# Small transfers of the attention stage issued by GpSimd in place of SyncE, in a trunk step of three-pass float32 products

## The chip, the cores and the metric

The kernel runs on one core of a Trainium2 chip. The metric is the device time of one launch in microseconds (us). PE is TensorE, PEld its weight loads, DVE is VectorE, ACT is ScalarE, POOL is GpSimd and SP is SyncE, which does nothing but issue transfers (DMAs) and wait. Each engine works through its own instructions in the order in which they stand; an instruction that waits holds up all that stand behind it on that engine.

## The reference

One inference step of two layers for 256 prompt tokens and 8 sample tokens that share the weights: attention and a gated MLP with a short convolution, then a state-space layer (S5) and such an MLP again. The change lies in the attention, which is cut down here to what matters:

```python
q, k, v = qkv_project(h, w_qkv, pos)          # partial rotary on q and k
for g, (win, dil) in enumerate(((128, 1), (512, 4), (2048, 16))):
    k_all = concat([cache_k[g], k[:, :, g]])  # prompt rows: no cache
    v_all = concat([cache_v[g], v[:, :, g]])
    o, lse = dilated_attend(q[:, :, g], k_all, v_all, idx, dil, win // dil)
o = merge_by_denominator(outs, lses)          # over the three groups
return o @ w_o, new_rows                      # the new k and v are outputs too
```

There are 8 heads in each of 3 groups, of 128 channels. The rotated keys and the values of all tokens are outputs.

## The kernel before

All activations lie transposed: channels on the 128 partitions, the 264 tokens along the free dimension. The weights stream through in chunks of eight 128x128 blocks (512 KB). SP loads a chunk (`wraw`, line 175), ACT rounds it to its high part (`whi`, line 162), DVE subtracts to get the rest (`wlo`, line 163), and PE makes three products of each block (lines 202 to 204), 24 to a chunk. There are four buffers for `wraw` and three each for `whi` and `wlo`.

The QKV product runs over the heads: first the keys of a head (three tiles, one for each group g), then the next head's queries, then the head's values. Work on a finished tile is put off by some chunks of weights (`later`), so that it comes between the big products; a scheduler then sets the final order on each engine.

- A finished key or query tile: DVE scales it out of PSUM (`qkv`, line 437) and shuffles 32 rows of it (`sw`, line 443). POOL makes the rotary from that in three operations (lines 449 to 451), which I call the rope. A query's rope ends with a copy `qe` (line 454) that PE reads (line 481); a key's with a small product `qk` (line 522). PE multiplies prompt queries and keys at lines 639 and 640, and its order there is fixed.
- Line 457 stores the rotated key tile to `out_kv` (132 KB), 24 times.
- The sample rows of a head: 24 dot products on DVE give `sc` (line 497). They are laid out anew through DRAM: `sc` is written to `sd` (line 505) and read back as `ss` on 8 partitions (line 510). DVE takes their maximum (`mgs`, line 536), the softmax follows, and the weights `ss` go back the same way: written to `pd` (line 554), read as `pk` on 128 partitions (line 597) for the sums over the cached values (lines 619 and 621). Each of the four is 12 KB, and each read waits for its write to land. There are 8 of each.
- In the background, a few small operations to each chunk, DVE and POOL make tables for the state-space layer (`z_room`, line 912).

Of the kernel before, what the change touches and what calls it, by code (L numbers as in the profile page):

```python
"""One inference step of the dilated-attention / S5 / ConvFFN trunk on one core.

All activations are held transposed: channels on the partitions, the 264 tokens (256 prompt, 8 sample) on
the free dimension.  Weights stream through in blocks of [128 x 128] and are the stationary operand.  A
float32 product is carried by three float32r passes: each operand is split exactly into a high part H
(float32r) and the rest L, and H*H + H*L + L*H is accumulated in PSUM.
"""
# [59 lines left out]
def order_grouped(mts, nk, first):  # L67
    """(k, m) blocks: the first `first` M-tiles k-outer, the others one after the other."""
    out = [(k, m) for k in range(nk) for m in mts[:first]]
    out += [(k, m) for m in mts[first:] for k in range(nk)]  # L70
    return out


def qkv_mtiles():
    """Keys of a head, the next head's queries, then the head's values."""
    seq = [(0, 0)]
    for h in range(H):
        seq += [(1, h)] + ([(0, h + 1)] if h + 1 < H else []) + [(2, h)]
    return [(which * G + g) * H + h for which, h in seq for g in range(G)]
# [24 lines left out]
class Put:  # L104
    """Notes calls to an engine for later."""
# [8 lines left out]
class Pin:  # L114
    """Calls to an engine that keep their place in its queue."""
# [8 lines left out]
class Kern:  # L124
# [12 lines left out]
    # ---------------------------------------------------------------- work put off by some chunks of weights  # L137
# [10 lines left out]
    # ---------------------------------------------------------------- helpers  # L148
# [16 lines left out]
    def ensure(self, i):  # L165
        """Load and split the weight chunks up to number i of the whole stream."""
# [13 lines left out]
    def gemm(self, name, order, nk, rhs, evac, lag=0):  # L180
        """Accumulate all blocks of `order`; rhs(k) -> (H, L) moving operands; evac(m, psum).
        The first output is taken out of PSUM `lag` chunks late, and at most two per chunk while catching up."""
# [31 lines left out]
    def ready(self, lst, k):  # L214
        """lst[k], running the put-off work until it is there."""
        while k >= len(lst) or lst[k] is None:
            self.pump()
        return lst[k]

    # ---------------------------------------------------------------- norms  # L220
    def rstd_mean(self, parts, warm=0):
        """-1/2 (mean of squares + eps) of every token, tokens on the partitions: [88, 3] in PSUM."""
# [11 lines left out]
    def rstd_root(self, mh):  # L234
        """2/3 of 1/sqrt(-2 mh): the bit-shift estimate, a step of third and a step of second order."""
# [18 lines left out]
    def rstd_spread(self, w):  # L254
        """[88, 3] -> a PSUM tile with 3/2 of every token's value on all partitions."""
        nc = self.nc
        ps = self.ps()
        for b in range(3):
            nc.tensor.matmul(
                ps[:, b * TB : (b + 1) * TB], w[:, b : b + 1].to_broadcast([TB, P]), self.ident15,  # L260
                start=True, stop=True,
            )
        return ps[:, 0:NT]

    def warm(self, n):
        """Keeps the tensor engine's clock up over a wait: n products that nothing reads."""
# [8 lines left out]
    def rstd_soon(self, acc):  # L275
        """Puts 1/rms of the squares in acc off into the coming chunks; returns the tile that will hold it."""
# [13 lines left out]
    def squares(self, st, x):  # L290
        """st: list with the running sum of squares (made here) and the tile still to be added."""
# [10 lines left out]
    def yevac(self, ys, gi):  # L302
        """Takes a sub-layer's output out of PSUM, times the post-norm's gain; sums its squares."""
# [10 lines left out]
    def reload(self, src, wait):  # L314
        """The residual, loaded tile by tile in the coming chunks."""
# [11 lines left out]
    def operand(self, x, gi, k):  # L327
        """H/L parts of x*g (not yet scaled by 1/rms); the L part is returned as a function."""
# [10 lines left out]
    def residual(self, ys, xs, sq, keep, gi):  # L339
        """x += rms_norm(y)*g tile by tile; then the next sub-layer's operand (gain gi), its squares, the store.  # L340
        Returns rhs(k) and the tile for 1/rms."""
# [45 lines left out]
    # ---------------------------------------------------------------- constants  # L387
# [18 lines left out]
    # ---------------------------------------------------------------- attention  # L406
    def attention(self, ap, rhs, rget):
        """Returns the list that will hold the split o^T tiles, one per head."""
# [16 lines left out]
        def both(what, h, fn):  # L425
            """Runs fn when the second of its two conditions is met."""
# [21 lines left out]
        def rope(which, g, h, t, sw):  # L448
# [7 lines left out]
            else:  # L456
                self.later(2, lambda: nc.sync.dma_start(O["kv"][0, g, h], t))
# [17 lines left out]
    def sample_q(self, ap, st, h, g):  # L475
        """The 8 sample queries, each on 16 partitions; scores of the cached keys, 8 to a partition."""
# [27 lines left out]
        def write():  # L504
            nc.sync.dma_start(self.sd[h].rearrange("b k g e -> (b k) (g e)"), sc.rearrange("p g e -> p (g e)"))
            self.later(2, read)

        def read():
            ss = ap.tile([NS, 16, G, 8], F32, tag="ss", name=self.nm("ss"), bufs=2)
            nc.sync.dma_start(ss, self.sd[h])  # L510
# [7 lines left out]
    def sample_new(self, ap, st, h, g):  # L518
        """Products of the sample queries with their own new keys."""
# [6 lines left out]
    def sample_softmax(self, ap, st, h):  # L526
        """Softmax weights of the sample queries over the three groups' cached and new keys."""
# [19 lines left out]
        def fin():  # L547
# [6 lines left out]
            nc.sync.dma_start(self.pd[h], ss)  # L554
# [7 lines left out]
    def merge_exp(self, ap, n, tag, mg):  # L562
        """exp(SCALE*(group max - joint max)); mg is [n, groups] or [n, blocks, groups]"""
# [14 lines left out]
    def merge(self, ap, n, tag, e, l, h):  # L578
        """Merge weight of each group over head 0's sum of that group (as the reference divides)."""
# [13 lines left out]
    def sample_out(self, ap, st, h):  # L593
        """Sum of the cached and new values with the softmax weights."""
        nc, I = self.nc, self.I
        pk = ap.tile([P, G, 8], F32, tag="pk", name=self.nm("pk"), bufs=2)
        nc.sync.dma_start(pk.rearrange("p g e -> p (g e)"), self.pd[h].rearrange("b k g e -> (b k) (g e)"))
# [36 lines left out]
    def prompt_scores(self, ap, st, h, g):  # L634
        """Masked scores of one group and their exponentials (against the group's maximum)."""
# [40 lines left out]
    def prompt_out(self, ap, st, h, os_):  # L676
        """P transposed group by group, and o^T accumulated over the groups."""
# [6 lines left out]
        def tr(g):  # L684
            # column blocks: (keys 0, queries 0), (keys 0, queries 1), (keys 1, queries 1)
# [23 lines left out]
    # ---------------------------------------------------------------- ConvFFN  # L709
    def ffn_prep(self, fp, l):  # L710
        """Convolution weights, and the part of the sample rows' convolution that the stored rows give."""
# [67 lines left out]
    # ---------------------------------------------------------------- S5  # L779
    def s5_setup(self, p):  # L780
        """What the state-space layer needs of every state: decay, phase, powers of a.  SN small steps at a time."""
# [20 lines left out]
        def exp(out, x):  # L802
            """e**x for x clamped to [-87, 88], to float32's accuracy."""
# [19 lines left out]
        # sin and cos: reduce to [-pi, pi], take a quarter of the angle, double twice  # L823
# [30 lines left out]
        # powers a**1..a**4: pw[:, 0] real, pw[:, 1] imaginary, pw[:, 2] minus imaginary  # L854
# [7 lines left out]
        # (a - 1) / lambda  # L862
# [17 lines left out]
        # unit phase w of a**4, its powers w**0..w**7 and w**0, w**8, .., w**56  # L880
# [37 lines left out]
    def s5_prep(self, p):  # L918
        """Chunk operators of the state-space layer (4 steps at once), kept in DRAM until they are used."""
# [14 lines left out]
        def finish(j):  # L934
            """Input operators with (channel, step) rows; Re(c a**k bbar) with k = 3 - step."""
# [20 lines left out]
        def finish2(j):  # L956
            """Operators from step s to step t of a chunk: Re(c a**(t - s) bbar) for s <= t."""
# [11 lines left out]
        def load_bc(j):  # L969
            """b and c of four pairs of groups: [p, (b_re b_im c_re c_im), t, 16]"""  # L970
# [14 lines left out]
        for j in range(KD):  # L985
# [6 lines left out]
            # phase tables w**i, i = 0..63  # L992
# [23 lines left out]
            for ri in range(2):  # L1016
                # re: c_re a_re - c_im a_im;  minus im: c_re (-a_im) - c_im a_re
# [15 lines left out]
    def s5(self, p, rhs, rget):  # L1033
# [9 lines left out]
        for ri in range(2):  # L1043
            # a * (initial sample state)
# [9 lines left out]
        def front(j, ps):  # L1054
            """u tile in (step, chunk) order, and through DRAM to (channel, step) rows."""
# [31 lines left out]
        def inject(j, up, u4, op, e, d0):  # L1087
            """What each chunk adds to the state."""
# [12 lines left out]
        def scan(j, up, u4, e, d0, pj):  # L1101
            """Rotate each chunk's share back by the phase, scan with the real decay, rotate again."""
# [88 lines left out]
    # ---------------------------------------------------------------- the step  # L1191
    def run(self):
# [18 lines left out]
        def ffn_layer(l, rhs, rget, keep, nxt):  # L1211
            with ExitStack() as s:
# [8 lines left out]
                def gpool(m):  # L1221
                    """Space for the last gated tiles is that of the state-space layer's preparation."""
# [39 lines left out]
    def first(self, ap, src):  # L1262
        """The first sub-layer's operand, straight from the input."""
# [32 lines left out]
# -------------------------------------------------------------------- host: layouts only  # L1296
# [11 lines left out]
def chan(a):  # L1308
    """[..., channels] -> [channel % 128, ..., channel // 128]"""
# [3 lines left out]
def constants():  # L1313
# [15 lines left out]
    # shift[(i c s'), t, (c s)]: 1 where s' = 3 - t + s  # L1329
# [6 lines left out]
def host_in(a):  # L1336
# [25 lines left out]
    def pl(v):  # L1362
        """[128 groups, 64, ...] -> [128 = (group % 2, state), 64 = group // 2, ...]"""
# [10 lines left out]
    # c of two groups side by side, each on its own group's rows: [j, p, t, (re im), (group, 16)]  # L1374
# [19 lines left out]
def host_out(o):  # L1394
# [8 lines left out]
    def unpl(v):  # L1403
        """[128, 64, ...] -> [128 groups, 64, ...]"""
# [28 lines left out]
```

## Time and profile before

| | |
|---|---|
| median of three runs | 2557.86 us |
| the three runs | 2555.21, 2557.86, 2563.43 us |
| span of the profiled execution | 2555.1 us |
| PE busy | 2469.9 us (97%) |
| DVE, ACT, POOL busy | 1817.1, 1159.4, 830.0 us |

The page gives the profiled execution by its span from the first to the last instruction, 2555.1 us; the shortest of the three runs is 2555.21 us, so next to nothing lies around it. A wait is read as "engine line waited for: us in total, times, longest us". In a row of instructions the bracket at the end is the idle time of the engine just before, and what ended it. The attention stage is roughly the first 530 us.

### The profile page before, as it was taken

The page shows a single profiled execution, that of the slowest core. Times are in us where ns is not written, and L with a number is a line of the kernel's source. Part 1 is how long each engine was busy: PE and PEld are TensorE (multiplying, and loading weights), DVE is VectorE, ACT ScalarE, POOL GpSimd, SP SyncE. Part 2 cuts the span into 40 slices and gives each one's busy share as a digit, 9 for nine tenths or more (in the row PEclk, how much of TensorE's full clock was granted, in tenths as well). Part 3 has the DMA queues.
Part 4 walks back from the last instruction along what each step waited for, and adds up shares of the span by engine and source line. Part 5 has one row for each costly group of instructions (what it writes and reads, how often), then busy time and mean ns, then how long its engine had stood idle before and what let it go on. Part 6 is the DMA issues. An engine that isn't in the chain of part 4 may idle for free.

```text
span 2555.1 us, 52974 instructions
## 1 busy us (share of the span) xinstructions
PE 2469.9 (97%) x20998; PEld 2440.6 (96%) x20998; DVE 1817.1 (71%) x3490; ACT 1159.4 (45%) x1754; POOL 830.0 (32%) x1153
## 2 busy tenths in 40 slices
PE   8999999999999999999999988999999999999997
PEld 8999998999999999999999988999999999999997
DVE  6787998778988887764445878445977777764444
ACT  5344433445555555443334333444655545543332
POOL 6333347344899990011003465102100000011001
PEclk9999999999999999999999999999999999999999
DMA  7666666666666665566556677555655555566553
GB/s 274 218 234 220 210 216 203 202 213 218 202 217 217 207 217 189 182 205 199 182 181 213 212 248 240 184 181 168 198 180 179 181 181 182 182 205 200 181 182 117
DMA packets 186874, 512.14 MB, mean 200 GB/s; under 512 B 39281, under 2 KB 68993, under 8 KB 186369
## 3 DMA queue, kind: packets, MB, share of 16 engines
q1 hardware_dynamic: 141808, 457.89, 54.2%
q0 software_dynamic: 7968, 26.71, 3.3%
q10 hardware_dynamic: 36848, 24.16, 3.2%
q8 instruction: 164, 2.69, 0.4%
q14 instruction: 86, 0.70, 0.1%
HBM read 469.80 MB, written 38.88 MB: 199 GB/s over the span
## 4 chain that ended last, share of the span: by engine, by line
PE 77%; DVE 11%; issue 4%; DMA 3%; ACT 2%; POOL 1%; ACTq 1%; SPq 0%; DVEq 0%; POOLq 0%
PE ps L202 25%; PE ps L204 25%; PE ps L203 24%; DVE wlo L163 4%; DMA yb<-y 1%; DVE C L744 1%; ACT whi L162 1%; DVE ac L621 1%; DVE act L367 1%; DMA ident<-in_ident 1%; ACTq L945 0%; POOL qkv L449 0%; DMA y<-yb 0%; DVE z_room L912 0%; DVE act L335 0%
## 5 line engine op out<-in xcount | busy, mean ns | idle before, releaser
L204 PE MATMUL ps<-act,wlo 128*128 128x264 f32 x6176 | 1763.6, 286 | 30.2 <-DVE wlo L163 30.0
L202 PE MATMUL ps<-act,whi 128*128 128x264 f32 x6176 | 1771.1, 288 | 10.6 <-ACT whi L162 8.3
L203 PE MATMUL ps<-act,whi 128*128 128x264 f32 x6176 | 1760.3, 285 | 10.0 <-DVE act L335 9.8
L163 DVE TENSOR_TENSOR wlo<-wraw,whi 128x1024 fp32r<-128x1024 f32 (+1 forms) x775 | 994.2, 1283 | 555.7 <-ACT whi L162 554.6
L162 ACT ACTIVATE whi<-wraw 128x1024 fp32r<-128x1024 f32 (+1 forms) x775 | 815.9, 1055 | 1024.7 <-PE ps L203 800.5
L204 PEld LDWEIGHTS ps<-act,wlo 128*128 128x128 f32 x6176 | 1168.7, 189 | 36.9 <-DVE wlo L163 36.8
L202 PEld LDWEIGHTS ps<-act,whi 128*128 128x128 f32 x6176 | 1166.1, 189 | 16.3 <-ACT whi L162 9.1
L203 PEld LDWEIGHTS ps<-act,whi 128*128 128x128 f32 x6176 | 1169.2, 189 | 13.0 <-DVE act L335 12.2
L294 POOL TENSOR_TENSOR acc<-acc,sq 128x264 f32<-128x264 f32 x112 | 111.3, 993 | 672.8 <-ACT sq L300 670.3
L736 POOL COPY ckeep<-U 128x10 f32<-128x10 f32 x172 | 64.4, 375 | 652.5 <-DVE U L735 651.4
L744 DVE SCALAR_TENSOR_TENSOR C<-U,cw,C 128x255 f32<-128x255 f32 (+1 forms) x344 | 187.7, 547 | 0.7 <-ACT C L738 0.7
L735 DVE TENSOR_TENSOR U<-ps,rstd 128x264 f32<-128x264 f32 x172 | 73.2, 430 | 72.2 <-PE ps L204 71.8
L738 ACT ACTIVATE C<-U,cw 128x264 f32<-128x264 f32 x172 | 102.1, 596 | 17.6 <-DVE U L735 13.1
L449 POOL TENSOR_TENSOR qkv<-qkv,cs 32x264 f32<-32x264 f32 x48 | 57.3, 1194 | 148.7 <-DVE sw L443 47.4
L121 POOL TENSOR_TENSOR z_e<-z_pa,z_pb 128x256 f32<-128x256 f32 x64 | 73.1, 1142 | 5.0
L621 DVE SCALAR_TENSOR_TENSOR ac<-vc,pk,ac 128x128 f32<-128x128 f32 x184 | 69.0, 375 | 2.2
L497 DVE CUSTOM_DVE_ANT_0 junk<-kc,qx 128x128 f32<-128x128 f32 x192 | 58.4, 304 | 1.4
L660 ACT ACTIVATE S<-S,nmg 128x128 f32<-128x128 f32 (+1 forms) x48 | 21.5, 447 | 82.0 <-DVE nmg L655 82.0
L451 POOL TENSOR_TENSOR qkv<-qkv,sw 32x264 f32<-32x264 f32 x48 | 56.4, 1176 | 3.4
L121 POOL TENSOR_TENSOR z_pa<-z_bc,z_tab 128x256 f32<-128x256 f32 x64 | 55.9, 874 | 2.4
L121 POOL TENSOR_TENSOR z_pb<-z_bc,z_tab 128x256 f32<-128x256 f32 x64 | 53.6, 838 | 0.0
L749 ACT ACTIVATE C<-C 128x264 f32<-128x264 f32 x86 | 35.7, 415 | 34.1 <-DVE C L744 30.4
(213 smaller groups left out, 1698.5 us busy)
## 6 DMA issues: line engine op xcount, KB each, us to landing
wraw<-in_w_up SPq DMA_DIRECT2D x344, 512.0 KB
wraw<-in_w_down SPq DMA_DIRECT2D x172, 512.0 KB
wraw<-in_w_qkv SPq DMA_DIRECT2D x143, 512.0 KB
wraw<-in_w_glu SPq DMA_DIRECT2D x64, 512.0 KB
wraw<-in_w_in SPq DMA_DIRECT2D x32, 512.0 KB
kc<-in_kc SPq DMA_DIRECT2D x24, 512.0 KB
vc<-in_vc SPq DMA_DIRECT2D x24, 512.0 KB
wraw<-in_w_o SPq DMA_DIRECT2D x16, 512.0 KB
```

The costliest lines, as they stand in the source:

```text
L121: return lambda *a, **k: self.tc.keep_in_program_order(getattr(self.eng, name)(*a, **k))
L162: self.nc.scalar.activation(hi, src, AF.Copy)
L163: self.nc.vector.tensor_tensor(lo, src, hi.bitcast(F32), op=ALU.subtract)
L202: nc.tensor.matmul(o, hi[:, c], xh, start=first, stop=False)
L203: nc.tensor.matmul(o, hi[:, c], xl, start=False, stop=False)
L204: nc.tensor.matmul(o, lo[:, c], xh, start=False, stop=last)
L294: nc.gpsimd.tensor_tensor(st[0], st[0], st[1], op=ALU.add)
L621: nc.vector.scalar_tensor_tensor(ac, vcs[g][:, e], w, ac, op0=ALU.mult, op1=ALU.add)
L735: nc.vector.tensor_tensor(u, ps[:, 0:NT], rget(), op=ALU.mult)
L736: nc.gpsimd.tensor_copy(keep[:, m, :], u[:, NP - 2 : NT])
L738: nc.scalar.activation(c, u, AF.Identity, bias=cw[:, 3, m : m + 1], scale=cw[:, 2, m : m + 1])
L744: nc.vector.scalar_tensor_tensor(c[:, s:NP], u[:, 0 : NP - s], cw[:, j, m : m + 1], c[:, s:NP], op0=ALU.mult, op1=ALU.add)
```

## The change

Five lines go from SP to POOL. The store of a new key (line 457) is also no longer put off by two chunks, but stands right behind the rope. Comments and docstrings are gone as well. Stores of values (line 462) and all big loads stay on SP.

```diff
             else:
-                self.later(2, lambda: nc.sync.dma_start(O["kv"][0, g, h], t))
+                nc.gpsimd.dma_start(O["kv"][0, g, h], t)
                 self.later(3, lambda: self.prompt_scores(ap, st, h, g))
                 self.sample_new(ap, st, h, g)
...
         def write():
-            nc.sync.dma_start(self.sd[h].rearrange("b k g e -> (b k) (g e)"), sc.rearrange("p g e -> p (g e)"))
+            nc.gpsimd.dma_start(self.sd[h].rearrange("b k g e -> (b k) (g e)"), sc.rearrange("p g e -> p (g e)"))
             self.later(2, read)
...
-            nc.sync.dma_start(ss, self.sd[h])
+            nc.gpsimd.dma_start(ss, self.sd[h])
...
-            nc.sync.dma_start(self.pd[h], ss)
+            nc.gpsimd.dma_start(self.pd[h], ss)
...
-        nc.sync.dma_start(pk.rearrange("p g e -> p (g e)"), self.pd[h].rearrange("b k g e -> (b k) (g e)"))
+        nc.gpsimd.dma_start(pk.rearrange("p g e -> p (g e)"), self.pd[h].rearrange("b k g e -> (b k) (g e)"))
```

SP has 998 rows before and 942 after, POOL 1140 and 1196. PE's order is the same, tile names aside. The numbers behind names count buffers and differ between the two kernels.

On SP, the first place where a stored key stands among the weight loads, the keys of head 0 (`qkv_694`, `qkv_738`, `qkv_742` are its groups 0, 1, 2). Before:

```order
L175 DMA wraw_799<-in_w_qkv 128x1024
L457 DMA out_kv<-qkv_694 128x264
L457 DMA out_kv<-qkv_738 128x264
L175 DMA wraw_852<-in_w_qkv 128x1024
L457 DMA out_kv<-qkv_742 128x264
L175 DMA wraw_897<-in_w_qkv 128x1024
```

And of the change:

```order
L175 DMA wraw_757<-in_w_qkv 128x1024
L797 DMA z_room<-in_lre 128x64
L797 DMA z_room<-in_lim 128x64
L797 DMA z_room<-in_ldt 128x64
L175 DMA wraw_802<-in_w_qkv 128x1024
L175 DMA wraw_854<-in_w_qkv 128x1024
L175 DMA wraw_897<-in_w_qkv 128x1024
```

The weight loads follow one another with no store between them.

On POOL, the keys of head 6: the rope of group 0, the tables of the state-space layer, the rope of group 1. Before:

```order
L451 TENSOR_TENSOR qkv_5824<-qkv_5824,sw_5826 32x264
L522 TENSOR_TENSOR qk_5856<-qkv_5236,qkv_5824 128x8
L912 TENSOR_TENSOR z_room<-z_room 128x64x2
L912 TENSOR_TENSOR z_room<-z_room 128x128 x2
L912 TENSOR_TENSOR z_room<-z_room 128x64x2
L912 TENSOR_TENSOR z_room<-z_room 128x256 x2
L912 TENSOR_TENSOR z_room<-z_room 128x64x4
L912 TENSOR_TENSOR z_room<-z_room 128x256
L449 TENSOR_TENSOR qkv_5957<-qkv_5957,cs 32x264
```

And of the change:

```order
L451 TENSOR_TENSOR qkv_5824<-qkv_5824,sw_5826 32x264
L457 DMA out_kv<-qkv_5824 128x264
L522 TENSOR_TENSOR qk_5857<-qkv_5237,qkv_5824 128x8
L912 TENSOR_TENSOR z_room<-z_room 128x64x2
L912 TENSOR_TENSOR z_room<-z_room 128x128 x2
L505 DMA sd_111<-sc_5406 128x24
L912 TENSOR_TENSOR z_room<-z_room 128x64x2
L912 TENSOR_TENSOR z_room<-z_room 128x256 x2
L912 TENSOR_TENSOR z_room<-z_room 128x64x4
L912 TENSOR_TENSOR z_room<-z_room 128x256
L510 DMA ss_6065<-sd_111 8x384
L449 TENSOR_TENSOR qkv_5958<-qkv_5958,cs 32x264
```

The store, the write of `sd` and the read of `ss` now stand on POOL ahead of the rope of group 1, and five table operations stand between the write and the read.

On DVE, the same place: the maximum `mgs` of head 6 among the work on its group 1 key (`qkv_5957` before, `qkv_5958` after). Before:

```order
L163 TENSOR_TENSOR wlo_5929<-wraw_5927,whi_5928 128x1024
L437 TENSOR_TENSOR qkv_5957<-ps_5874,rstd_528 128x264
L443 STREAM_SHUFFLE sw_5959<-qkv_5957 32x264
L163 TENSOR_TENSOR wlo_5987<-wraw_5985,whi_5986 128x1024
L536 TENSOR_REDUCE mgs_6198<-ss_6064 8x3
L163 TENSOR_TENSOR wlo_6032<-wraw_6030,whi_6031 128x1024
```

And of the change:

```order
L163 TENSOR_TENSOR wlo_5930<-wraw_5928,whi_5929 128x1024
L437 TENSOR_TENSOR qkv_5958<-ps_5875,rstd_528 128x264
L536 TENSOR_REDUCE mgs_6198<-ss_6065 8x3
L443 STREAM_SHUFFLE sw_5960<-qkv_5958 32x264
L163 TENSOR_TENSOR wlo_5988<-wraw_5986,whi_5987 128x1024
L163 TENSOR_TENSOR wlo_6033<-wraw_6031,whi_6032 128x1024
```

The maximum stands one shuffle and one weight split earlier. It moves in the same way in head 2; in head 3 it moves ahead of the key's lines 437 and 443; in heads 1, 4, 5 and 7 it stays where it was.

## Rows read from the trace of the kernel before

**Rows 1.** The page, busy us and share of the span by engine.
```profile
PE 2469.9 (97%) x20998; PEld 2440.6 (96%) x20998; DVE 1817.1 (71%) x3490; ACT 1159.4 (45%) x1754; POOL 830.0 (32%) x1153
```
**Rows 2.** Waits of PE between 60 and 510 us: total, times, longest.
```profile
PE ps L204 <- DVE wlo L163: 20.8, 17, 2.7
```
**Rows 3.** Stretches: length, then PE, PEld, DVE, ACT, POOL busy, granted clock, DMA share, GB/s.
```profile
60.00:110.00 50.00, 47.26 (x376) 45.73 (x375) 36.74 (x151) 20.26 (x35) 21.80 (x31) 1.00 0.65 218
...
140.00:150.00 10.00, 8.44 (x47) 8.44 (x48) 9.93 (x32) 3.77 (x7) 4.23 (x6) 0.66 0.67 229
410.00:420.00 10.00, 7.00 (x45) 6.58 (x45) 10.00 (x30) 2.39 (x3) 8.41 (x15) 0.86 0.55 192
...
500.00:510.00 10.00, 8.08 (x52) 7.78 (x51) 6.81 (x16) 2.88 (x6) 6.39 (x7) 0.83 0.29 83
```
**Rows 4.** Waits of DVE between 60 and 510 us.
```profile
DVE mgs L536 <- DMA ss<-sd: 29.0, 6, 7.9
```
**Rows 5.** Instructions in order of time, 66 to 73 us: start, us, engine, line.
```profile
66.00 0.34 SPq L457 DMA_DIRECT2D out_kv<-qkv  x1
...
70.34 1.06 ACT L162 ACTIVATE whi<-wraw 128x1024 fp32r<-128x1024 f32 x1 [8.96 <-DMA wraw<-in_w_qkv]
...
72.96 0.39 PE L204 MATMUL ps<-act,wlo 128*128 128x264 f32 x1 [0.93 <-DVE wlo L163]
```
**Rows 6.** Instructions in order of time, 71 to 76 us, POOL and PE.
```profile
71.90 1.60 POOL L451 TENSOR_TENSOR qkv<-qkv,sw 32x264 f32<-32x264 f32 x1
...
73.56 0.29 POOL L454 COPY qe<-qkv 128x128 f32<-128x128 f32 x1
...
75.74 0.49 PE L481 MATMUL ps<-ident,qe 128*128 128x128 f32 x3
```
**Rows 7.** POOL's transfers, line 320, then line 1164 (landing): min/median/max.
```profile
L320 POOL DMA_DIRECT2D act<-xd x48: 536/536/553, 1137.2 to 2321.8; - x48
...
DMA to landing us min/median/max: 2.4/4.6/8.1
...
DMA to landing us min/median/max: 2.1/2.1/2.1
```
**Rows 8.** SP's issues in order of time, heads 2, 6 and 7.
```profile
175.68 0.40 SPq L505 DMA_DIRECT2D sd<-sc  x1
...
434.22 0.38 SPq L505 DMA_DIRECT2D sd<-sc  x1
...
496.18 0.34 SPq L457 DMA_DIRECT2D out_kv<-qkv  x1
496.62 0.38 SPq L505 DMA_DIRECT2D sd<-sc  x1
...
500.40 0.28 SPq L510 DMA_DIRECT2D ss<-sd  x1
```
**Rows 9.** The maximum on DVE in heads 2, 6 and 7, in order of time.
```profile
183.59 0.54 DVE L536 TENSOR_REDUCE mgs<-ss 8x3 f32<-8x384 f32 x1 [4.74 <-DMA ss<-sd]
...
439.58 0.54 DVE L536 TENSOR_REDUCE mgs<-ss 8x3 f32<-8x384 f32 x1 [4.50 <-DMA ss<-sd]
...
501.89 0.54 DVE L536 TENSOR_REDUCE mgs<-ss 8x3 f32<-8x384 f32 x1 [7.86 <-DMA ss<-sd]
```
**Rows 10.** POOL in order of time, head 6.
```profile
433.83 1.31 POOL L522 TENSOR_TENSOR qk<-qkv,qkv 128x8 f32<-128x8 f32 x1
435.11 4.76 POOL L912 TENSOR_TENSOR z_room<-z_room 128x128 f32<-128x128 f32 x8
439.83 2.03 POOL L449 TENSOR_TENSOR qkv<-qkv,cs 32x264 f32<-32x264 f32 x1
...
442.65 0.76 POOL L451 TENSOR_TENSOR qkv<-qkv,sw 32x264 f32<-32x264 f32 x1
```
**Rows 11.** PE in order of time: head 6's scores of group 1, and a wait in head 7.
```profile
443.47 0.49 PE L639 MATMUL ps<-qkv,qkv 128*128 128x128 f32 x2
...
504.41 0.39 PE L204 MATMUL ps<-act,wlo 128*128 128x264 f32 x1 [1.92 <-DVE wlo L163]
```

## Prediction

> **What bounds the kernel now.** First the page by engines: PE is busy for 97% of the span, DVE for 71%, POOL for 32% [rows 1]. So PE sets the time, and only what makes PE wait can be won or lost. The change touches the attention stage alone, so next I read who PE waits for between 60 and 510 us: 17 waits for DVE's weight split `wlo`, 20.8 us in all [rows 2]. The stretches add the clock: where PE had stood still for long, the granted clock is 0.66, 0.86 and 0.83 in a stretch of 10 us [rows 3], which at the lower level (1.2 in place of 2.4 GHz) gives 3.4 + 1.4 + 1.7 = 6.5 us of lost PE time. That makes about 27 us, 1.1% of the time: no relief of this stage can bring more.
>
> Why is DVE late? In two of these stretches it is 99% busy and more [rows 3], but it also stands still for 29.0 us, in 6 waits, at the maximum `mgs` until the scores come back from DRAM [rows 4]. DVE time lost there is missing later. Once, the weights themselves are late: at 66 us SP stands at a key's store that waits for POOL's rope, the next weight load stands behind it, ACT idles 8.96 us for those weights, and PE waits 0.93 us at 72.96 [rows 5].
>
> **The change part by part.** The sum is made against the profiled execution, 2555.1 us, which lies 2.8 us under the median.
>
> SP loses 24 stores and 32 small transfers, 56 rows. That frees weight loads, and pays where a load was late, which the trace shows at the start alone. PE stands still for 50 - 47.26 = 2.7 us between 60 and 110 us [rows 3], and I put all of that down to the late load. Against it, POOL issues three stores more in the same rush of ropes, 0.54 us each [rows 7], and weight splits that now run earlier on DVE fall on ropes: beside a split a rope's operation took 1.60 us [rows 6] where one alone takes 0.76 [rows 10]. The last `qe` of this rush is done at 73.85 us, and PE reads it at 75.74 [rows 6]. With 1.6 + 0.8 us more it is done at 76.3, while PE without its first wait comes at 74.8: a new wait of 1.5 us. Net **-1.2 us** (bounds -2.7 and +1).
>
> The round trip of the scores. No small transfer of POOL is in the trace, so I bound one by its others: it lands 2.1 us after its issue at the least (64 KB, line 1164) and 4.6 in the median (132 KB, line 320) [rows 7]. 12 KB is nearer to the former; I take 3.0. Two in a row are 6.0 us, 4.2 to 9.2. Before, from the issue of the write to the maximum, it was 7.9 us in head 2, 5.4 in head 6 and 5.3 in head 7 [rows 8, 9]. So there is hardly a gain in the transfer itself; it comes 0.54 us later because POOL issues the key's store first. POOL also has to wait until the write has landed before it can issue the read, some 2.5 us, with the next group's rope queued behind. That rope waits for the next key's tile anyhow, one chunk of weights and more after the last (head 6 alone shows it in my rows, 6 us from 433.8 to 439.8 [rows 10]), so I cost this wait at nothing; what it costs without that cover is the second rival. By place:
> - Heads 2 to 5: the maximum may start up to a us earlier, but in heads 2 and 3 the shuffle of the next key stands behind it, and one or two splits. I take **-1.0 us** for the four together (bounds -8 and +14; see the rivals).
> - Head 1: one more store ahead of the read and the longer landing: **+1.0 us** (0 to +3).
> - Head 7: the write is now ahead of the rope, so it has landed when the rope is done. The read leaves right behind the store and `qk`, at 496.2 + 0.5 + 0.2 = 497.0 us, in place of 500.40 [rows 8]. It lands at 500.0; the maximum came at 501.89 [rows 9]. DVE is 1.9 us earlier, and PE's wait of 1.92 us at 504.41 [rows 11] goes, and with it the lost clock of 1.7: 3.6 us, of which I take **-3.0** because the write's own issue now delays the rope.
> - Head 6: here POOL's queue hurts. The rope of group 0 ends at 433.8 us; then the store (0.5), `qk` (1.3), three of the eight table operations (4.76 x 3/8 = 1.8), so the write of `sd` goes at 437.4 in place of 434.22. The other five operations take 3.0, so the read of `ss` goes at 441.0 and lands at 444.0; the maximum ran at 439.58 [rows 8 to 10]. The shuffle now stands behind the maximum, the rope of group 1 behind the shuffle: maximum 0.54 [rows 9], the shuffle (an estimate) not more than that, rope 2.3 (three times 0.76) to 3.6 (as before, 439.8 to 443.4) [rows 10], and it ends between 447.4 and 448.7. PE wants it at 443.47 [rows 11]: a new wait of 3.9 to 5.2 us, I take 4.4, and 1.7 for the clock as at 504 us. **+6.1 us** (bounds +2.8, if the landing is 2.1 and the clock holds, and +9).
>
> The way back of the weights (`pd`, `pk`): the write waits on POOL for DVE's last scaling, the read for the write's landing. Behind them stands the third query's rope, wanted several us later; I cost this at nothing, at a wait of 1 us a head if that cover is gone. Value stores and loads on SP are unchanged.
>
> Sum: -1.2 + 1.0 - 1.0 + 6.1 - 3.0 = +1.9 us, 2557.0 against the profiled 2555.1, or **2559.5** against the median. A measurement of this kernel tells a change of 0.3% (7.7 us) from none, so I forecast no change that can be told.
>
> The transfers on SP's queue took unequal times: head 7's read some 1.5 us (500.40 to 501.89), while of head 2's two, 7.9 us together, one took 3.9 or more [rows 8, 9]. The Trainium skill, "DMA: Bandwidth & Descriptors", section Queues, rings and completion order, says that each DMA engine goes round the queues that have work, a packet at a time; so a small transfer on another queue need not stand behind the weights on SP's. No row here shows a small one on POOL's queue. By that rule the landing is at its lower end, and the first rival below comes out.
>
> POOL's 48 issues of line 320 took 536 to 553 ns throughout [rows 7], with DVE at work beside them. Against the change speaks the Trainium skill, "SBUF — State Buffer", section SBUF: two separate sides: the descriptors of a POOL transfer are written by GpSimd and starve while certain copies on DVE hold the port that both share. The even issue times don't bear it out, but these 48 lie outside the attention; by that rule the third rival below comes out.
>
> **The rivals.**
> - *The round trip gets short.* If small transfers land in 2.1 us, each head's scores are 1.8 us earlier than I took. For: 12 KB is little. Against: nothing of POOL's landed faster. Heads 1 to 5 hold some 16 us of PE's waits and 4.8 of lost clock; I let half the waits (8) and all of that clock go. -1.2 - 8 - 4.8 + 3 (head 6) - 3.6 = -14.6: **2543 us**.
> - *POOL's waits for its own writes take the place of SP's* (slower). The mechanism is one: POOL stands still until a write lands, the next rope stands behind, and PE behind the rope. If landings are 4.6 us, the median of line 320, the pair takes 3.2 us more than I took. Heads 1 to 5 then cost some 2.5 us each (12.5) and the clock twice (3.4), head 6 7.7, head 7 brings nothing: -1.2 + 12.5 + 3.4 + 7.7 = +22: **2580 us**. It decides from a landing of about 3.8 us on. For: transfers of POOL in the busy stretches; against: these were ten times as large.
> - *Issues on POOL are held up by DVE.* 7 issues a head, each 0.9 us longer, of which some 1.5 us a head end on the rope that PE waits for: 8 x 1.5 = 12 on top of the sum: **2572 us**. Against: the even issue times.
>
> **How the numbers follow.** Forecast 0.60 (its own range 2551 to 2565); short round trip 0.13; POOL's waits 0.20; held issues 0.07. Faster by over 0.3%, under 2550.2: 0.13 and a little of the forecast's edge, 0.14. Slower, over 2565.5: 0.26. Same: 0.60. The range reaches from 2546 to 2577: it leaves out about half of each outer case.
>
> **What would show it.** Right: SP's weight load near 66 us is issued by 58 us, and ACT's wait of 8.96 us is gone; PE's waits for `wlo` before 110 us shrink; a new wait of PE on the rope in head 6 of 3 to 5 us, with a drop of the clock behind it; no wait of that kind in head 7, and no lost clock there. DVE's wait at the maximum stays near 29 us in all, longer in head 6 (about 10 us) and shorter in head 7. Wrong: landings of POOL's small transfers under 2.3 or over 3.8 us; PE waiting for ropes in most heads; issues on POOL over 0.6 us; or the total of PE's waits in this stage outside 15 to 30 us.

## The result: 0.65% slower, by way of VectorE and not of the ropes

The changed kernel takes 2575.9 us (median of 4 runs, 2571.1 to 2581.4), the kernel before 2558.4 on the same chip: a ratio of 1.0065, 95% interval 1.0047 to 1.0083, some 17 us. The time lies inside the range given, near its upper end; the likeliest case, no change that can be told, did not come. The second rival had forecast 2580, but for another reason than the one that the profile shows. Of the six runs of e1 below, one took 2968.3 us and five took 2545.9 to 2556.4; its row goes by the five.

### The profile page after: what moved, and what is told of

It is laid out like the page before. It is cut to its first block, busy times and chain, and to the rows that moved or that the text cites. A ratio compares the mean times of both kernels' runs of the same rounds, so it can differ in the third digit from the quotient of the medians.

```text
span 2575.5 us, 52966 instructions
## 1 busy us (share of the span) xinstructions
PE 2478.1 (96%) x20998; PEld 2447.5 (95%) x20998; DVE 1819.1 (71%) x3490; ACT 1160.1 (45%) x1754; POOL 856.3 (33%) x1209
## 3 DMA queue, kind: packets, MB, share of 16 engines
q1 hardware_dynamic: 135792, 454.25, 53.9%
## 4 chain that ended last, share of the span: by engine, by line
PE 66%; DVE 6%; DMA 3%; issue 3%; ACT 2%; POOL 1%; ACTq 1%; SPq 0%; DVEq 0%; POOLq 0%
PE ps L203 21%; PE ps L202 21%; PE ps L204 21%; DVE wlo L163 2%; DMA yb<-y 1%; DVE C L744 1%; ACT whi L162 1%; DMA y<-yb 1%; ACTq L945 1%; DVE act L367 0%; PE ps L961 0%; DVE act L335 0%; ACT z_ow L941 0%; PE ps L272 0%; DVE C L756 0%
## 5 line engine op out<-in xcount | busy, mean ns | idle before, releaser
L760 DVE TENSOR_TENSOR act<-C,act 128x264 fp32r<-128x264 f32 x86 | 49.8, 580 | 1.2 <-ACT act L758 1.2
```

## The profile after

The page by engines answers to [rows 1]: the span is 20.4 us longer. PE's busy time is 8.2 us longer for the same matmuls, about what it lost in addition at the lower clock: 5.1 us in the attention stage and 3.6 behind it.

```profile
span 2575.5 us, 52966 instructions
...
PE 2478.1 (96%) x20998; PEld 2447.5 (95%) x20998; DVE 1819.1 (71%) x3490; ACT 1160.1 (45%) x1754; POOL 856.3 (33%) x1209
```

PE's and DVE's waits between 40 and 560 us (total, times, longest), against [rows 2] and [rows 4]:

```profile
DVE mgs L536 <- DMA ss<-sd: 48.1, 8, 8.4
PE ps L204 <- DVE wlo L163: 28.5, 18, 4.6
...
PE ps L608 <- DVE dg L552: 2.4, 1, 2.4
PE ps L481 <- POOL qe L454: 2.2, 1, 2.2
PE ps L639 <- POOL qkv L451: 0.5, 2, 0.2
```

DVE stands still at the maximum for 48.1 us in place of 29.0, in all 8 heads in place of 6. PE waits 28.5 us for DVE's weight splits in place of 20.8. For the ropes it waits 2.7 us in all (0.5 at line 639, 2.2 for `qe`), where before there was no such row: little of the time is lost that way.

Stretches, against [rows 3] (columns as there; 518 to 528 is head 7's, the former 500 to 510):

```profile
60.00:110.00 50.00, 47.85 (x375) 47.02 (x374) 39.67 (x151) 20.49 (x35) 24.78 (x36) 0.97 0.64 216
188.00:198.00 10.00, 7.81 (x50) 7.76 (x51) 8.63 (x20) 3.09 (x7) 8.35 (x8) 0.83 0.43 127
...
455.00:465.00 10.00, 5.88 (x27) 5.88 (x28) 6.69 (x15) 2.73 (x6) 7.15 (x9) 0.66 0.35 120
518.00:528.00 10.00, 8.83 (x69) 8.42 (x68) 6.51 (x16) 3.36 (x8) 5.93 (x7) 1.00 0.35 118
```

Head 2 in order of time shows how a wait of DVE becomes one of PE (against [rows 8, 9]):

```profile
180.15 0.56 POOL L505 DMA_DIRECT2D sd<-sc  x1
...
186.30 0.54 POOL L510 DMA_DIRECT2D ss<-sd  x1 [5.59 <-DMA sd<-sc]
188.11 0.54 DVE L536 TENSOR_REDUCE mgs<-ss 8x3 f32<-8x384 f32 x1 [7.63 <-DMA ss<-sd]
...
188.59 0.43 DVE L443 STREAM_SHUFFLE sw<-qkv 32x264 f32<-32x264 f32 x1
188.93 2.34 DVE L163 TENSOR_TENSOR wlo<-wraw,whi 128x1024 fp32r<-128x1024 f32 x2
...
190.19 0.39 PE L204 MATMUL ps<-act,wlo 128*128 128x264 f32 x1 [3.88 <-DVE wlo L163]
```

The write's landing alone takes 5.9 us. The maximum waits 7.63 us on DVE (4.74 before), and two splits stand behind it, one of them because of the place that the change gave it. PE stands still for 3.88 us, and its clock then falls: the 10 us from 188 have a granted clock of 0.83, where the kernel before had no loss.

Head 6, against [rows 9 to 11]:

```profile
449.20 0.58 POOL L457 DMA_DIRECT2D out_kv<-qkv  x1 [0.30 <-POOL qkv L451]
...
451.27 0.59 POOL L505 DMA_DIRECT2D sd<-sc  x1
...
451.88 3.35 POOL L912 TENSOR_TENSOR z_room<-z_room 128x128 f32<-128x128 f32 x5
...
455.17 0.54 POOL L510 DMA_DIRECT2D ss<-sd  x1
457.05 0.54 DVE L536 TENSOR_REDUCE mgs<-ss 8x3 f32<-8x384 f32 x1 [8.43 <-DMA ss<-sd]
...
457.87 2.34 DVE L163 TENSOR_TENSOR wlo<-wraw,whi 128x1024 fp32r<-128x1024 f32 x2
458.09 2.73 POOL L449 TENSOR_TENSOR qkv<-qkv,cs 32x264 f32<-32x264 f32 x1 [2.37 <-issue]
...
459.12 0.59 PE L204 MATMUL ps<-act,wlo 128*128 128x264 f32 x1 [4.64 <-DVE wlo L163]
```

POOL's order is the one foretold, store, `qk`, three table operations, write, five more, read. But PE comes to a stand at a weight split behind the maximum, before it wants the rope.

The transfers on POOL: issue times (ns, min/median/max) of `sd` and `ss`, then the landings of both (us). Line 457's 132 KB stores are in the second fence.

```profile
L505 POOL DMA_DIRECT2D sd<-sc x8: 563/576/587, 91.6 to 510.9; - x8
L510 POOL DMA_DIRECT2D ss<-sd x8: 524/530/542, 96.6 to 516.4; - x8
...
DMA to landing us min/median/max: 1.8/3.9/5.9
```

```profile
L457 POOL DMA_DIRECT2D out_kv<-qkv x24: 565/588/624, 62.5 to 531.5; - x24
...
DMA to landing us min/median/max: 2.1/3.8/6.1
```

12 KB land no sooner than 132 KB.

## The experiments

**Theory**: the scores come back later, the maximum stands earlier on DVE, and the splits behind it are late for PE. **Rivals**: the key stores or POOL's own standing delay the ropes; the way back (`pd`, `pk`) costs; `sd` stands behind the 132 KB store.

For each kernel: ratio to the kernel before with its 95% interval; DVE's wait at `mgs`; PE's standing still (sum of its gaps over 0.15 us from 40 to 560 us) plus the clock lost there (half of the time at 1.2 GHz); and the *way of the scores*, from the end of a head's last dot product to the landing of `ss`, summed over the 8 heads. It has four legs: to the issue of `sd`, its landing, the issue of `ss`, its landing. The last two columns are added up from the trace, which holds one execution of each kernel; the ratio is to runs of the kernel before made beside it (medians of 2557.9 to 2559.3 us).

| kernel | median us | ratio | `mgs` | PE still + clock | way |
|---|---|---|---|---|---|
| before | 2558.4 | 1 | 29.0 | 21.7 + 6.8 | 66.5 |
| changed | 2575.9 | 1.0065 [1.0047, 1.0083] | 48.1 | 33.8 + 11.9 | 78.5 |
| e1 keys only | 2549.8 | 0.9964 [0.9952, 0.9976] | 17.2 | 16.5 + 5.1 | 58.9 |
| e2 small only | 2577.8 | 1.0074 [1.0062, 1.0086] | 47.1 | 34.3 + 13.7 | 77.5 |
| e3 scores on SP | 2547.2 | 0.9958 [0.9946, 0.9970] | 15.4 | 15.4 + 1.7 | 53.9 |
| e4 weights on SP | 2578.5 | 1.0078 [1.0066, 1.0090] | 56.0 | 38.5 + 11.9 | 83.8 |
| e5 max later | 2566.4 | 1.0027 [1.0014, 1.0040] | 39.2 | 26.6 + 8.5 | 77.8 |
| e6 SP, max late | 2548.9 | 0.9961 [0.9947, 0.9974] | 3.1 | 14.7 + 5.1 | 56.4 |
| e7 POOL, max late | 2556.7 | 0.9989 [0.9980, 0.9997] | 14.6 | 18.4 + 6.8 | 82.8 |
| e8 write on SP | 2572.8 | 1.0049 [1.0036, 1.0063] | 42.7 | 32.3 + 5.1 | 74.2 |
| e9 keys later | 2558.3 | 0.9996 [0.9985, 1.0007] | 29.5 | 19.1 + 6.8 | 63.6 |
| e10 keys behind | 2544.4 | 0.9946 [0.9931, 0.9961] | 15.9 | 13.4 + 3.4 | 55.1 |
| e11 before, max late | 2546.3 | 0.9950 [0.9934, 0.9966] | 6.0 | 16.5 + 3.4 | 68.1 |
| e12 behind, max late | 2543.5 | 0.9940 [0.9921, 0.9958] | 4.6 | 15.9 + 0.0 | 57.1 |

### Which part costs: e1 to e4

Of the changed kernel's five edits, e1 keeps the key stores, e2 the four small transfers; e3 takes `sd` and `ss` back, e4 `pd` and `pk`. For e3:

```
-            nc.gpsimd.dma_start(self.sd[h].rearrange(...), ...)
+            nc.sync.dma_start(self.sd[h].rearrange(...), ...)
...
-            nc.gpsimd.dma_start(ss, self.sd[h])
+            nc.sync.dma_start(ss, self.sd[h])
```

> Only the 24 key stores are on GpSimd, the four small transfers a head are on SyncE as before. The loss to explain is 17 us: about 12 us more of PE standing still between 40 and 560 us and 5 us of lost clock. Theory (the scores' way out and back, sd and ss, on GpSimd's queue, and the earlier place of the maximum on VectorE that goes with it): 2558 us, within 3 us of before, DVE's wait at mgs in all about 29 us. Rival one (the key stores delay the ropes): about 2575. Rival two (the way back of the weights, pd and pk): 2558. Rival three (sd stands in one DMA queue behind the 132 KB key store): 2558, since sd goes by another queue here.

> Only the small transfers are on GpSimd, the key stores are on SyncE and two chunks late, as before. Theory: 2575 us, as after, with the maximum mgs waiting near 48 us in all. Rival one (key stores): 2558. Rival two (pd and pk): 2575. Rival three (sd behind the key store in one queue): 2560, the landings of sd fall from a median near 4.2 to under 3.5 us, and the wait at mgs falls to 35 us or less.

> Key stores and the way back of the weights (pd, pk) on GpSimd, the scores' way (sd, ss) on SyncE. Theory: 2558 us, mgs waits back at about 29 us. Rival one (key stores): 2575. Rival two (pd and pk): 2575. Rival three (sd behind the key store): 2558.

> Key stores and the scores' way (sd, ss) on GpSimd, the way back of the weights (pd, pk) on SyncE. Theory: 2574 us, as after, mgs waits near 46 us. Rival one (key stores): 2575. Rival two (pd and pk): 2558. Rival three (sd behind the key store): 2574.

The scores' way is the cost: with both of its transfers on POOL 2576 to 2579, whatever else moves, with it on SP 2547 to 2550. So rivals one and two fall (e4 is no faster than the changed kernel, and e1 and e3 can't be told apart). Rival three falls with e2, which is slow without a key store on POOL's queue. The theory's 2558 for e1 and e3 missed too: the key stores alone are a gain of 9 us. The SP queue's waits (total, times, longest) of before, of e1 and of the later e10 show where the gain may come from:

```profile
SPq L457 <- POOL qkv L451: 81.8, 18, 9.5
...
SPq L457 <- POOL qk L522: 18.6, 5, 5.0
```

```profile
SPq L175 <- DVE wlo L163: 116.1, 51, 5.7
```

```profile
SPq L457 <- POOL qkv L451: 5.3, 6, 2.4
```

Before, SP stood some 82 us at key stores until a rope was done, with the write of the scores behind in some heads; in e1 it has no such row, and its largest is that of the weight loads, which wait for a free buffer (60.2 us before). The first leg of the way, from the last dot product to the issue of `sd`, is 15.1 us in all before, 3.5 in e1, and 9.9 in the changed kernel, where `sd` stands behind POOL's work instead.

### Place or arrival: e5 and e8

e5 is the changed kernel with the maximum held behind a named instruction, so that DVE's order is that of e3 in every row:

```
-        nc.vector.tensor_reduce(mg, ss..., op=ALU.max)
+        self.behind(nc.vector.tensor_reduce(mg, ss..., op=ALU.max), {0: self.dotted[-3], 2: self.cuts[-5], 3: self.turns[-3], 6: self.cuts[-5]}.get(h))
```

`dotted`, `cuts` and `turns` note the dot products, weight splits and shuffles. e8 moves the write `sd` alone back to `nc.sync`.

> The changed kernel, with the maximum mgs held on VectorE behind the same instruction as in e3_scores_on_sync, in heads 0, 2, 3 and 6 (one to three places later); VectorE's order is then that of e3_scores_on_sync in every row, and the two differ only in who issues the scores' two transfers. e3_scores_on_sync took 2547 us, the changed kernel 2576. If the earlier place of the maximum is the whole cost: 2549 us. If the later arrival of the scores is (8 round trips, 78.5 us in all in place of 53.9): 2573. Both, about half each: 2562, with the wait at mgs near 32 us.

> The changed kernel with only the write of the scores (sd) back on SyncE; the read (ss), pd, pk and the key stores stay on GpSimd, and VectorE's order is that of the changed kernel in every row. If the write's own way (its place behind ropes and stores in GpSimd's queue, its landing) makes up half of the 25 us by which the eight round trips got longer: the sum of the round trips falls from 78 to about 65 us, time 2563. If the read's place and landing on GpSimd are the cost: 2574.

With the order put right, 9.5 us of the 29 between e3 and the changed kernel go (by the ratios, 10 of 27); the other 19 stay, and these two kernels differ only in who issues `sd` and `ss`. Both are at work, and between these two the later arrival more. The time lies between the forecasts for an even split (2562) and for the arrival alone (2573). Against the kernel before it reads otherwise: e5 has that kernel's place of the maximum in every head but head 3, and putting the order right gives back 9.5 of the 17 us that the change costs. Not all that stays goes by way of the splits, since PE also waits 6.3 us for ropes in e5 (4.0 in e3), most of it here:

```profile
PE ps L639 <- POOL qkv L451: 4.2, 3, 3.0
```

e8 missed its first theory: the legs to the write's landing shrink from 9.9 + 33.4 to 3.1 + 23.2 us, but POOL gets to the read later (8.3 to 14.3 us) and it lands later (26.9 to 33.7); 4 us of way are won, and 3 of time, which the two intervals do not tell apart.

### Is it DVE's standing still? e6, e7, e11 and e12

These hold the maximum at least one split further back in heads 2 to 7: e6 on e3, e7 on the changed kernel (and head 0 as in e5), e11 on the kernel before.

```
+        self.behind(nc.vector.tensor_reduce(mg, ss..., op=ALU.max), self.cuts[-4] if h > 1 else None)
```

> The changed kernel with the same holding back of mgs as in e6_sync_max_late, for head 0 as in e5_max_later. Theory (VectorE stands still at mgs because the scores come late, and the weight splits behind it are late for PE): the wait at mgs falls from 48 to about 20 us, the time from 2576 to about 2556. Rival (GpSimd's own standing still, with the ropes behind it, is what costs): the wait at mgs falls as well, but the time stays within 5 us of 2575.

> e3_scores_on_sync (2547 us) with the maximum mgs held one weight split further back on VectorE in heads 2 to 7, behind the masks of the next group. If VectorE's standing still at mgs is what makes PE wait: the wait at mgs falls from 15 to under 6 us and the time to 2541. If it is covered by then: 2547. If the softmax then comes too late for what follows: slower, 2552.

> The kernel before, with nothing moved to GpSimd, and the maximum mgs held one weight split further back on VectorE in heads 2 to 7, as in e6_sync_max_late. If VectorE's standing still at the maximum costs PE time whoever issues the transfers: the wait at mgs falls from 29 to under 8 us, PE's standing still from 22 to about 15 us, and the time from 2558 to 2551. If in the kernel before this wait is covered, and only SyncE's standing at the key stores costs: 2558.

e7 decides against POOL's standing as the main cause. Its waits from 40 to 560 us:

```profile
POOL sd L505 <- DVE sc L497: 20.1, 4, 6.5
POOL pk L597 <- DMA pd<-ss: 18.2, 7, 5.0
...
DVE mgs L536 <- DMA ss<-sd: 14.6, 6, 4.8
PE ps L204 <- DVE wlo L163: 12.2, 10, 2.7
POOL ss L510 <- DMA sd<-sc: 8.9, 3, 4.4
POOL ss L510 <- DVE mg L651: 5.6, 1, 5.6
```

POOL still stands for most of what it did (52.8 us at `sd`, `ss` and `pk`, 62.5 in the changed kernel), and the way of the scores is even longer (82.8), but DVE meets the maximum later and waits 14.6 us; 19 of the changed kernel's us come back. Some 8 remain against e6, which has the same order on DVE in every row and differs in who issues `sd` and `ss`. PE's waits for ropes (5.1 us in e7, 2.9 in e6) are a part of them; the rest is not shown. e11 shows the worth of the place without POOL: SP stands at the key stores as before (the first fence, its SP queue's waits; the second has PE's and DVE's), the way is 68.1, and the later place alone gives 11.6 us. With the maximum late in both, the changed kernel (e7) is still some 10 us behind the kernel before (e11), so the change keeps a cost that the place does not remove.

```profile
SPq L457 <- POOL qkv L451: 73.4, 17, 7.7
```

```profile
PE ps L204 <- DVE wlo L163: 14.8, 12, 2.7
...
DVE mgs L536 <- DMA ss<-sd: 6.0, 3, 4.2
```

e6 missed its first expectation: with 12 us less of DVE's wait than e3, PE stands as long, and the time is the same. With the scores on SP, the last 12 us of the wait cost nothing that could be told; PE's other 15 us of standing still come from elsewhere.

### SP freed without POOL: e9, e10, e12

```
-                self.later(2, lambda: nc.sync.dma_start(O["kv"][0, g, h], t))
+                self.later(6, lambda: self.tc.keep_in_program_order(nc.sync.dma_start(O["kv"][0, g, h], t)))
```

That is e10, which holds the store behind all that SP was given earlier; e9 has the `6` alone; e12 adds e11's place of the maximum.

> The kernel before, all on SyncE, with the key stores put off by six chunks of weights in place of two. e1_keys_only, with the key stores on GpSimd, took 2551 us against 2559 before. If that gain came because SyncE stood at a key's store until the rope was done, with the write of the scores behind it: the first leg of the round trips (last dot product to the issue of sd) falls from 15.1 us in all to under 6, and the time to about 2551. If it came from anything else that GpSimd's queue brings (stores on another queue, fewer issues on SyncE): the time stays at 2559.

> All transfers on SyncE as before, with the key stores not only put off by six chunks but held in SyncE's queue behind what was recorded ahead of them, so that in every head the write of the scores stands ahead of the next key's store, and one weight load or more lies between a rope and its store. If the gain of e1_keys_only (2551 against 2559) came because SyncE stood at a key's store with sd behind it: SyncE's waits at the key stores for the rope fall from 82 us to under 20, the first leg of the round trips from 15 to under 6, and the time to 2551. If GpSimd's queue brought it in another way: 2558, although SyncE stands no more.

> e10_keys_behind (2544 us) with the maximum mgs held back in the same way. In e10 the wait at mgs is down to 16 us, and below that e6_sync_max_late showed no gain: 2544 again, within 4 us, with the wait at mgs under 5 us. If the last 13 us of PE's standing still hang on it: 2538.

e9 did not take away what it should: its stores stood in nearly the same places on SP, which still waited 66.6 us (17 times) at them. It says nothing on the cause. e10 did (the 5.3 us above), the first leg is 3.2 us, and the time of 2544.4 beats the 2551 foretold, without anything on POOL. That the whole gain is the scores' earlier arrival isn't shown apart from the weight loads, which go earlier too, nor from the maximum of head 7, which the scheduler set one split later in e1 and e10 (though not in e3, which gains as much as e1). e12, the fastest median, is no faster than e10 or e11 that could be told: either remedy takes what there is.

## Why the prediction went wrong, by its steps

The time lies 1 us inside the end of the range, which reached there on account of the rivals; the sum gave +1.9 us and 17 came, so that it fell inside is luck. The steps, by PE's standing still and lost clock (each loss of clock counted with the wait ahead of it):

- *Start, -1.2.* The late weight load is gone (SP issues it at 55.3 us), and so is ACT's wait of 8.96 us; the foretold new wait for `qe` came, 2.15 us for 1.5. Not foretold was that the clock falls behind it (0.97 in the stretch, 1.7 us). PE's gaps are 0.5 us shorter: +1.1 in all, just outside the bound of +1.
- *Head 1, +1.0.* Between 110 and 180 us PE stands still for 5.4 in place of 4.7 us, at the same lost clock: +0.7.
- *Heads 2 to 5, -1.0.* This is the step that failed. From 180 to 390 us PE stands 14.0 us in place of 6.5 and loses 3.4 us of clock in place of none: +10.9, inside the bounds of -8 and +14. It held that the maximum "may start up to a us earlier" and set no price on the splits behind it; DVE waits there 7.6, 7.7, 3.2 and 4.5 us in place of 4.7, 6.5, 1.1 and none. Head 2 alone has 5.6 of the 10.9 us (3.9 of standing and 1.7 of clock, none before), and its scores came no later: 9.1 us behind the last dot product, 9.4 before. DVE came to the maximum sooner, 1.5 us behind that dot product in place of 4.7. With the order put back (e5) PE loses 1.4 us in head 2. In heads 4 and 5, where the maximum kept its place, the way of the scores grew, from 6.1 and 7.1 to 8.1 and 10.9 us.
- *Head 6, +6.1.* From 390 to 480 us +5.2 of standing and +1.7 of clock, +6.9. The size came out, by luck: PE waits for a split and not for the rope.
- *Head 7, -3.0.* -0.7 and -1.7, -2.4: the clock loss went, as foretold, but not for the reason given. The write left POOL 0.3 us behind the last dot product, the read only at 516.37, 3.4 us after the write had landed, and the way of the scores is 0.6 us longer than before (9.6). Why PE waits less there is not shown.
- *Way back at nothing.* Held: e4 is no faster than the changed kernel.

These add up to 17.2 us; the rest of the span's 20.4 is clock lost behind the stage, which no run ties to the change. Beneath heads 2 to 5 lie two things. One is a mis-sized term, the landing: 3.0 us taken, 3.9 measured, because I put 12 KB nearer to the 64 KB row than to the 132 KB one. The trace before spoke against going by size, and against the sentence that it held no small transfer of POOL: one of 8 KB landed in 3.8 us, behind the attention stage, and 512 KB took no longer.

```profile
st_e<-z_e POOLq DMA_DIRECT2D x16, 512.0 KB, 3.9
...
dsk<-in_dskip POOLq DMA_DIRECT2D x1, 8.0 KB, 3.8
```

By the prediction's own limit of 3.8 us that is the second rival's side. Its price (2580) nearly came, its mechanism did not: PE waits 2.7 us for ropes, and e7 takes most of the loss away while POOL stands on. The other thing is the order on DVE, 99% busy in two stretches [rows 3]. The prediction named the splits behind the maximum in heads 2 and 3, but reckoned only when the scores arrive, and not when DVE comes to wait for them; the new order has the maximum earlier in four heads (0, 2, 3 and 6; the section on the change leaves out head 0). Of the signs of being wrong two came, the landing of 3.9 us and 33.8 us of PE's waits. Two sums are off a little: +1.9 us on the median makes 2559.8, not 2559.5, and the read in head 7 comes out at 496.9, not 497.0.

The Trainium skill's rule ("DMA: Bandwidth & Descriptors", Queues, rings and completion order) that each DMA engine goes round the queues that have work, from which the prediction took that a small transfer on its own queue need not stand behind the weights, did not bring the lower end here: the least landing is 1.8 us, the median 3.9. The other ("SBUF — State Buffer", SBUF: two separate sides), that POOL's descriptors starve while certain operations of DVE hold a port that both share, doesn't show in the issues: those of the scores and the stores took 524 to 624 ns with DVE at work. Whether DVE ran such operations beside them is not shown here.

## What to carry to other kernels

Moving a transfer to a less busy engine's queue frees the old queue only of what it stood waiting for; ask what waits at the far end, and how long that end may be late. An instruction that waits for a DRAM round trip on a busy in-order engine belongs behind the work that others need soon: here its place was worth as much (11.6 us) as clearing the queue ahead of the transfer (14). A store that waits for its data should not stand ahead of a transfer whose landing others wait for: on SP, holding the stores back gave those 14 us, though the weight loads also moved.

## What was not expected of the hardware

- On POOL's queue a 12 KB transfer landed in 1.8 to 5.9 us (median 3.9), a 132 KB store in 2.1 to 6.1 (median 3.8). What makes one landing short and the next long stays open; standing behind a key store is not it alone, since e2 has none and its scores took 1.8 to 5.1 us.
- SP's issue took 0.33 us for `sd` and 0.29 for `ss` in e3 (medians), POOL's 0.58 and 0.53 in the changed kernel: over 16 transfers that makes some 4 of the 11 us by which the landings of the changed kernel exceed e3's (60.3 against 49.1 in all).
- Behind PE's wait of 2.15 us for `qe`, at 77.39, the granted clock was the lower one (1.2 in place of 2.4 GHz) for 3.4 us: 1.7 us lost on top of the wait, in a place where I had priced the wait alone.
